# One weave instead of two for a hybrid streaming encoder step, with longer runs of value products and a sample hand-off through DRAM

## The chip, the cores and the metric

The kernel runs on one core of a Trainium2 chip. The metric is the device time of one execution in microseconds (us). Three timed executions of the kernel before gave 2235.5, 2245.63 and 2247.02 us, with a median of 2245.63 us. Engines are named as the profile names them: PE (matrix multiplies; PEld its weight loads), DVE (vector), ACT (scalar), POOL (GpSimd), SP (the queue that issues nearly all DMAs).

## The reference

One layer of a streaming encoder is computed for 2048 prompt tokens and for 8 sample streams of 16 tokens (17 blocks of 128 tokens; block 0 is the sample). Cut to what matters:

```python
h = rms_norm(x, g_in)
qkv_a, z_a, b_a, a_a, q_b, k_b, v_b, z_b, q_i, k_i, w_i, q_m, z_m = split_cols(h @ w_in)
# A: gated delta rule, 4 heads of 128, after a causal convolution; recurrent over chunks
o_a, s_new = gated_delta(q_a, k_a, v_a, g_log, beta, s0, chunk)
o_a = rms_norm(o_a, g_o) * silu(z_a)
# B: an indexer scores every admissible key, the best 256 of a query are attended to
score = einsum('bqh,bqhs->bqs', w_i, relu(einsum('bqhd,bsd->bqhs', q_i, k_i)))
_, idx = top_k(where(adm, score, -inf), 256)
o_b = softmax(q_b @ k_b[idx]) @ v_b[idx] * silu(z_b)      # the sample has 4096 cached keys a stream
# C: attention to 256 memory tokens
o_m = softmax(q_m @ mem_k) @ mem_v * silu(z_m)
y = x + concat(o_a, o_b, o_m) @ w_out
```

The outputs are y, the new convolution and recurrent states, and the new keys and values.

## The kernel before

**Order of the program.** The work is written as Python generators ("streams"). `weave` (lines 173 to 204) advances them by a clock of its own: each engine operation has an assumed cost (class `Paced`, lines 147 to 170, whose line 169 is the line under which the profile lists every compute instruction), and the stream with the smallest clock is asked for its next piece. The order in which instructions come out of this is their order of priority. The planner behind it then lays out each engine's queue: among instructions whose inputs it expects to be ready, the one that was written first goes first. An instruction of the second half can therefore stand in a queue ahead of a later-ready one of the first half. On the chip each queue runs in its order.

**First half** (`weave` at lines 1383 and 1384). `projections` multiplies the normalised input by the pieces of w_in (PSUM bank pair `pp`), group by group of three or four blocks, and writes q, k, v, gates and indexer queries to DRAM (`n_post`, `idx_post`). `stage_a`, `stage_b`, `stage_c` are the delta rule of each head and group (PSUM `pa`, `pb`, `pl`, `po`), whose results go to `mixT_d[0:512]` in DRAM; part of it is a small triangular inverse by 30 DVE steps with DMA round trips through DRAM (`blk_d`, lines 1074 to 1098). `index()` (1379) runs the memory keys, the sample's indexer and `idx_prompt` for the blocks 3 to `EARLY` - 1 = 13. After the weave the first half's pools (`b1`) are closed at line 1387.

**Second half** (`attention(True)`, lines 1695 to 1965, with a weave of its own at 1965, whose clocks begin at zero). Its pools take the memory of the closed ones: on the right side `sp` (the sample), `wo` and `op` (the output product), PSUM `py`; on the left side `kv`, `ap`, PSUM `pt`, `ps`, `po`. The right side of the first half holds what the projections use, the left side what the delta rule uses. A tile of a new pool waits for the tiles that were at its place. The streams are:

- `sample(M, sx)`: three streams. `keys_in` and `values_in` load the cached keys and values, `rows` (line 1540) goes through 72 steps of online softmax, 68 for the cache (`kind` 0) and 4 for the memory (`kind` 1). When the last of a kind is done, its result, which lies in `os_d` in DRAM, is gathered into rows by 32 small DMAs (lines 1671 to 1674), gated and written to `mix_d`. The tile for this is `work["PT"]`, which the next steps need too, and the generator stands at that place until the hand-off is over.
- `operands`, `scores`, `values`: attention of the prompt blocks 1 to 16, in order. `scores` writes exponentials into `Sm` slots; `values` (1834) transposes them four blocks at a time into PSUM `pt`, copies these to an SBUF buffer `PT` (three of them), and when three are waiting multiplies two (`visit`, 1837: four products of 128x64 by 128x128 for a buffer). `mixT` goes to `mixT_d[512:]`.
- `outputs` (1936): part 0 adds the delta rule's half of `w_out` to x and writes `part_d`; part 1 adds the attention's half and writes y. Each part loads and splits its half of w_out first (`split`, 1908), then goes through the blocks 1 to 16 and 0 at the end. A block is 24 matmuls in two PSUM banks.
- `late` (1726): `idx_prompt` for the blocks 14 to 16. When the indexer's last block is done, `more` (1730) lends its SBUF tiles to `Sm` slots and to the sample, the sample moves from PSUM `py` to the indexer's `pi`, and every other score bank is one of `pi`.

Should the selection have been inexact, the whole second half runs again (line 1980); it does not in these runs.

Of the kernel before, what the change touches and what calls it, by code (L numbers as in the profile page):

```python
# [5 lines left out]
F32 = mybir.dt.float32  # L6
# [13 lines left out]
NT = 17  # L20
# [11 lines left out]
EARLY = 14  # L32
NSEL = 256
PRI1 = (0, 0, 0, 0, 0, 0, 0, 0, 0, 0, 300, 0)
PRI2 = (0, 0, 0, 0, 0, 0, 0, 0, 0)
# [171 lines left out]
def build(tc, nc, a):  # L207
# [26 lines left out]
    os_d = dpool.tile([2, 4, 128, 64], F32, name="os_d")  # L234
    mix_d = scr("mix_d", [128, 512], F32)
# [27 lines left out]
    xpool = b1.enter_context(tc.tile_pool(name="xpool", bufs=1, side="right"))  # L263
    wpool = b1.enter_context(tc.tile_pool(name="wpool", bufs=2, side="right"))
# [21 lines left out]
    pp = b1.enter_context(tc.tile_pool(name="pp", bufs=2, space=PSUM, side="right"))  # L286
# [974 lines left out]
    np_ = b1.enter_context(tc.tile_pool(name="np", bufs=2, side="right"))  # L1261
    xp = b1.enter_context(tc.tile_pool(name="xp", bufs=XR, side="right"))
# [200 lines left out]
    class Slots:  # L1463
# [5 lines left out]
        def take(self, shape, dt, name):  # L1469
            place = self.free.pop(0)  # L1470
            return place[0].tile(shape, dt, name=name, tag=place[1], bufs=1), place
# [8 lines left out]
    def sample(M, sx):  # L1480
# [5 lines left out]
        one = M["any"]  # L1486
# [53 lines left out]
        def rows():  # L1540
# [68 lines left out]
            for j in range(n_ + 2):  # L1609
# [50 lines left out]
                if acc is not None and (c2 == 16 or kind2):  # L1660
# [7 lines left out]
                    if p2 == 3:  # L1668
                        og = work["PT"].rearrange("p a b c -> p a (b c)")
                        ot, gt = og[:, 0], og[:, 1]  # L1670
                        for h in range(4):
                            sv = os_d[kind2].rearrange("p (b h q) d -> p b h q d", b=2, h=4)[:, :, h].rearrange("p b q d -> (p b) q d")
                            for pb in range(8):
                                nc.sync.dma_start(ot[16 * pb:16 * pb + 16, 64 * h:64 * h + 64], sv[pb])  # L1674
                        nc.sync.dma_start(gt, gate_d[0:128, 256 * kind2:256 * kind2 + 256])
# [19 lines left out]
    def attention(first):  # L1695
        with ExitStack() as b3:
            nonlocal pt_, ps_, po_
            def pool(stack, name, bufs, **kw):
                return stack.enter_context(tc.tile_pool(name=name, bufs=bufs, reuse_waits="tile", **kw))
            sp = pool(b3, "sp", 1, side="right")  # L1700
            wo = pool(b3, "wo", 1, side="right")
            op = pool(b3, "op", 1, side="right")
            py = pool(b3, "py", 2, side="right", space=PSUM)
            kv = pool(b3, "kv", 1)
            ap = pool(b3, "ap", 1)
            pt_ = pool(b3, "pt", 2, space=PSUM)
            ps_ = pool(b3, "ps", 1, space=PSUM)
            po_ = pool(b3, "po", 1, space=PSUM)
            mkst = kv.tile([128, 4, 256], F32R, name="mkst")
            mvt = kv.tile([128, 2, 256], F32, name="mvt")  # L1710
            Kst = kv.tile([128, 4, 2048], F32R, name="Kst")
            Vt = kv.tile([128, 16, 256], F32, name="Vt")
            tiles = {g: {} for g in range(NT)}
            ready = []
            M = sample_tiles(sp)
            sms = Slots(*((ap, "Sm%d" % i) for i in range(NS)))
# [117 lines left out]
            def values():  # L1834


                def visit(po, nb, late, n):
                    lead = None
                    for hp, b, PT in late[:n]:
# [5 lines left out]
                        lead = ins  # L1845
                    del late[:n]

                for g in range(1, NT):
# [4 lines left out]
                    for part in range(2):  # L1853
# [3 lines left out]
                        for hp in range(2):  # L1857
# [9 lines left out]
                            for i in range(0, len(blocks), 4):  # L1867
# [7 lines left out]
                                PT = ap.tile([128, 4, 128], F32, name="PT", bufs=3)  # L1875
# [4 lines left out]
                                late.append((hp, b, PT))  # L1880
# [55 lines left out]
            def outputs():  # L1936
                for part in range(2):
                    w = yield from split(part)
                    for g in (*range(1, NT), 0):
                        rows = slice(g * 128, g * 128 + 128)  # L1940
                        if part:
                            yield from until(lambda: count["o"] >= g if g else done["smp"])
# [25 lines left out]
    attention(True)  # L1968
# [8 lines left out]
    with tc.If(clean == 0):  # L1977
        with tc.tile_pool(name="fp", bufs=2) as fp:
            exact_selection(fp)
        attention(False)  # L1980
# [33 lines left out]
```

## Time and profile before

| what | value |
|---|---|
| median of three timed executions | 2245.63 us (2235.5 to 2247.02) |
| profiled execution | 2253.76 us |
| its span, first to last instruction | 2252.0 us |
| mean granted clock of PE | 0.938 |
| DVE, ACT, POOL busy | 1661.6, 1284.3, 418.5 us |
| last projection matmul starts | 1453.0 us |
| last state of the delta rule is sent out (line 1386) | 1514.7 us |

The profile is of one execution. Busy times are sums over instructions of an engine; a matmul's end is modelled, so PE can be counted as busy while the next matmul could already start. A tile is named without its buffer number, and a name can stand for two pools (`po` is the delta rule's and later the attention's).

### The profile page before, as it was taken

What the parts mean: (1) busy time and instruction counts of PE and PEld (TensorE: products, weight loads), DVE (VectorE), ACT (ScalarE), POOL (GpSimd) and SP (SyncE); (2) the same over time, 40 slices, a digit from 0 to 9 for tenths busy, and PEclk for the clock granted to TensorE, in tenths of its full rate; (3) what the DMA queues carried; (4) which work ended last, traced back from release to release, by engine and by line L of the source; (5) the groups of instructions that cost most, each with busy time, mean ns of one, the idle gap of its engine ahead of it and who ended that gap; (6) DMA issues with size and microseconds to landing.
All of it is one profiled execution on the core that took longest, in us unless ns stands there. A gap on an engine that the chain in (4) does not pass through costs nothing.

```text
span 2252.0 us, 42965 instructions
## 1 busy us (share of the span) xinstructions
PE 1971.5 (88%) x13795; PEld 1607.3 (71%) x13795; DVE 1661.6 (74%) x6595; ACT 1284.3 (57%) x3337; POOL 418.5 (19%) x494
## 2 busy tenths in 40 slices
PE   4875978988789998999899999988999999999984
PEld 3654756877678887888788888846676666777752
DVE  5666867566888789999898999877677687655541
ACT  3455555455546566566667666557567577545430
POOL 3331423201120111111111011123211131111000
PEclk9996989889899999999899999979999999999996
DMA  7777777776544545565565755556766676765642
GB/s 236 186 228 227 269 182 214 192 253 201 185 160 158 188 164 201 207 232 187 190 230 201 244 195 189 169 176 217 246 204 219 218 228 200 242 210 185 195 139 82
DMA packets 323675, 453.21 MB, mean 201 GB/s; under 512 B 81776, under 2 KB 230896, under 8 KB 303984
## 3 DMA queue, kind: packets, MB, share of 16 engines
q1 hardware_dynamic: 323120, 449.32, 62.3%
q8 instruction: 111, 1.82, 0.3%
q0 software_dynamic: 320, 1.06, 0.2%
q14 instruction: 124, 1.02, 0.1%
HBM read 344.53 MB, written 105.75 MB: 200 GB/s over the span
## 4 chain that ended last, share of the span: by engine, by line
PE 37%; DVE 20%; DMA 6%; ACT 4%; issue 3%; SPq 1%; POOL 0%; DVEq 0%; ACTq 0%; POOLq 0%
PE py L169 10%; PE pp L169 6%; PE pt L169 5%; PE pi L169 4%; PE po L169 4%; DVE score L169 4%; PE ps L169 3%; PE pb L169 2%; DVE tmp L169 1%; PE pl L169 1%; ACT junk L169 1%; SPq L1674 1%; PE pa L169 1%; DMA svt<-in_v 1%; DVE k L169 1%
## 5 line engine op out<-in xcount | busy, mean ns | idle before, releaser
L169 PE MATMUL pp<-wh,xh 128*128 128x256 f32 (+1 forms) x952 | 292.6, 307 | 2.1 <-ACT wh L169 1.9
L169 PE MATMUL pp<-wl,xh 128*128 128x256 f32 (+1 forms) x952 | 281.3, 296 | 0.1
L169 PE MATMUL pp<-wh,xl 128*128 128x256 f32 (+1 forms) x952 | 278.6, 293 | 0.0
L169 PE MATMUL pp<-xh,wh 128*128 128x384 f32 (+1 forms) x640 | 246.7, 385 | 7.3 <-ACT q L169 4.6
L169 ACT ACTIVATE relu<-pi 128x512 f32<-128x512 f32 (+3 forms) x340 | 184.2, 547 | 107.2 <-PE pi L169 43.4
L169 PE MATMUL pp<-xl,wh 128*128 128x384 f32 (+1 forms) x640 | 239.4, 374 | 0.0
L169 PE MATMUL pp<-xh,wl 128*128 128x384 f32 (+1 forms) x640 | 238.4, 373 | 0.1
L169 DVE SCALAR_TENSOR_TENSOR score<-relu,w,score 128x512 f32<-128x512 f32 (+3 forms) x304 | 219.2, 722 | 15.5 <-ACT relu L169 7.8
L169 PEld LDWEIGHTS pp<-wh,xh 128*128 128x128 f32 x952 | 186.5, 196 | 6.7 <-issue 2.5
L169 ACT ACTIVATE junk<-score,tf 128x1024 bf16<-128x1024 f32 (+11 forms) x126 | 142.7, 1132 | 81.8 <-DVE tf L169 53.5
L169 PEld LDWEIGHTS pp<-wl,xh 128*128 128x128 f32 x952 | 186.7, 196 | 3.0 <-POOL wl L169 0.8
L169 PEld LDWEIGHTS pp<-wh,xl 128*128 128x128 f32 x952 | 186.0, 195 | 0.9
L169 PE MATMUL pi<-kstack,qst 128*128 128x512 f32 (+3 forms) x346 | 151.6, 448 | 35.7 <-DVE kstack L169 17.7
L169 POOL TENSOR_TENSOR Lm<-Lp,cf 128x256 f32<-128x256 f32 (+1 forms) x120 | 82.5, 688 | 327.1 <-PE pb L169 281.0
L169 PEld LDWEIGHTS pp<-xh,wh 128*128 128x128 f32 x640 | 125.2, 196 | 18.0 <-ACT q L169 5.6
L169 PEld LDWEIGHTS pp<-xl,wh 128*128 128x128 f32 x640 | 125.1, 195 | 9.4 <-issue 0.2
L169 PEld LDWEIGHTS pp<-xh,wl 128*128 128x128 f32 x640 | 123.6, 193 | 10.9 <-POOL wl L169 1.3
L169 PE MATMUL py<-woh,mixh 128*128 128x512 f32 x272 | 123.2, 453 | 7.4 <-ACT mixh L169 6.2
L169 PEld LDWEIGHTS pi<-kstack,qst 128*128 128x128 f32 x346 | 68.0, 198 | 67.8 <-ACT relu L169 30.1
L169 PE MATMUL py<-woh,mixl 128*128 128x512 f32 x272 | 110.8, 407 | 0.9 <-POOL mixl L169 0.9
L169 POOL TENSOR_TENSOR wl<-wr,wh 128x512 fp32r<-128x512 f32 (+1 forms) x61 | 80.6, 1330 | 164.5 <-ACT wh L169 153.8
L169 PE MATMUL py<-wol,mixh 128*128 128x512 f32 x272 | 110.5, 406 | 0.0
(428 smaller groups left out, 5352.3 us busy)
## 6 DMA issues: line engine op xcount, KB each, us to landing
skt<-in_kT SPq DMA_DIRECT2D x128, 256.0 KB
svt<-in_v SPq DMA_DIRECT2D x128, 256.0 KB
kraw<-in_kidxT SPq DMA_DIRECT2D x43, 256.0 KB
xres<-in_x SPq DMA_DIRECT2D x34, 256.0 KB
part_d<-xres SPq DMA_DIRECT2D x34, 256.0 KB
xres<-part_d SPq DMA_DIRECT2D x34, 256.0 KB
out_y<-xres SPq DMA_DIRECT2D x34, 256.0 KB
mixr<-mixT_d SPq DMA_DIRECT2D x33, 256.0 KB
```

The lines of the kernel that those rows point to most:

```text
L169: return f(*args, **kw)
L1674: nc.sync.dma_start(ot[16 * pb:16 * pb + 16, 64 * h:64 * h + 64], sv[pb])
```

## The change

The two weaves become one. `attention` now gets the first half's streams as `ahead` and weaves them together with its own. The pools of the first half are split in two stacks, `b2` (right side: projections) and `b1` (left side: delta rule). The stream `right` waits until the projections and their later steps are written out, closes `b2` and opens the second half's right pools; `left` waits for the last piece of the delta rule, sends out the two states, closes `b1` and opens the left pools. Every other stream of the second half is wrapped in `then`, which waits for its side. `index()` goes through all blocks up to 16; `late` and `EARLY` are gone.

In `values` the `PT` buffers become slots. Three are the old ones, two more are the indexer's `relu` buffers, lent when the indexer is done. When no slot is free, all waiting buffers but one are multiplied in one run: two of three as before, or four of five.

The gathering of the sample's result goes through a DRAM tile `ot_d`: four DMAs from DRAM to DRAM, one for a head, and one load of 128 rows of 1 KB take the place of 32 DMAs.

`outputs` goes through the blocks from 0 on. In part 0 the blocks 14 to 16 wait until the left side is open. If the next block is not ready (block 0 in part 1 until the sample is done), the one behind it is taken.

```diff
-    b1 = ctx.enter_context(ExitStack())
+    b1, b2 = (ctx.enter_context(ExitStack()) for _ in range(2))
...
     def index():
         yield from memory_keys(tp, pi)
         yield from idx_sample(tp, pi, SLOT)
-        yield from idx_prompt(range(3, EARLY), tp, pi, SLOT)
-    weave(tc, log, *zip((small_constants(), stage_c(), stage_b(), post(posts_t, "tp"), post(posts_n, "n"), stage_a(), splits(), loads(),
-          index(), cache_keys(), prep(xp), projections()), PRI1))
-    nc.sync.dma_start(a["pconv"], hist)
-    nc.sync.dma_start(a["pssm"].rearrange("h d e -> d h e"), Sst)
-    b1.close()
+        yield from idx_prompt(range(3, NT), tp, pi, SLOT)
...
                         for h in range(4):
-                            sv = os_d[kind2].rearrange("p (b h q) d -> p b h q d", b=2, h=4)[:, :, h].rearrange("p b q d -> (p b) q d")
-                            for pb in range(8):
-                                nc.sync.dma_start(ot[16 * pb:16 * pb + 16, 64 * h:64 * h + 64], sv[pb])
+                            nc.sync.dma_start(ot_d[kind2][:, 64 * h:64 * h + 64].rearrange("(c q) d -> c q d", q=16),
+                                              os_d[kind2].rearrange("p (b h q) d -> p b h q d", b=2, h=4)[:, :, h].rearrange("p b q d -> (p b) q d"))
+                        nc.sync.dma_start(ot, ot_d[kind2])
                         nc.sync.dma_start(gt, gate_d[0:128, 256 * kind2:256 * kind2 + 256])
...
+            def right():
+                nonlocal sp, wo, op, py
+                if first:
+                    yield from until(lambda: done["end"] and done["n"] == len(posts_n))
+                    b2.close()
...
+                done["right"] = 1
+
+            def left():
+                nonlocal kv, ap, pt_, ps_, po_, mkst, mvt, Kst, Vt, sms, pts
+                if first:
+                    yield from until(lambda: done["right"] and done["c"] == len(pieces_))
+                    nc.sync.dma_start(a["pconv"], hist)
+                    nc.sync.dma_start(a["pssm"].rearrange("h d e -> d h e"), Sst)
+                    b1.close()
...
+                pts = Slots(*((ap, "PT%d" % i) for i in range(3)))
+                done["left"] = 1
+
+            def then(side, stream):
+                yield from until(lambda: done[side])
+                yield from stream
...
-            def late():
-                if first:
-                    yield from idx_prompt(range(EARLY, NT), tp, pi, SLOT)
-
             def more():
-                yield from until(lambda: done["k"] == NT - 1)
+                yield from until(lambda: done["k"] == NT - 1 and done["left"])
                 sms.free += [(tp, "score"), (tp, "qst")]
+                pts.free += [(tp, "relu", 2)] * 2
...
-                    for hp, b, PT in late[:n]:
+                    for hp, b, (PT, place) in late[:n]:
...
                         lead = ins
+                        pts.free.append(place)
...
-                                if len(late) > 2:
-                                    visit(po, nb, late, 2)
+                                if not pts.free:
+                                    visit(po, nb, late, len(late) - 1)
...
-                    for g in (*range(1, NT), 0):
+                    left_ = list(range(NT))
+                    while left_:
+                        if part:
+                            ok = lambda g: count["o"] >= g if g else done["smp"] and done["left"]
+                        else:
+                            ok = lambda g: not first or g < 14 or done["left"]
+                        yield from until(lambda: ok(left_[0]) or len(left_) > 1 and ok(left_[1]))
+                        g = left_.pop(0 if ok(left_[0]) else 1)
...
-            weave(tc, log, *zip((more(), *sample(M, sx), values(), scores(), operands(), outputs(), late()), PRI2))
+            streams = [right(), left(), more(), *(then("right", s_) for s_ in sample(M, sx)),
+                       *(then("left", s_) for s_ in (values(), scores(), operands())), then("right", outputs())]
+            weave(tc, log, *zip(ahead, PRI1), *streams)
```

More of the change, by code (lines that the diff above doesn't have):

```diff
@@ L234, in build @@
     os_d = dpool.tile([2, 4, 128, 64], F32, name="os_d")
+    ot_d = dpool.tile([2, 128, 256], F32, name="ot_d")
     mix_d = scr("mix_d", [128, 512], F32)
@@ L285, in small_constants @@
         done["cn"] = 1
-    pp = b1.enter_context(tc.tile_pool(name="pp", bufs=2, space=PSUM, side="right"))
+    pp = b2.enter_context(tc.tile_pool(name="pp", bufs=2, space=PSUM, side="right"))
     pa = b1.enter_context(tc.tile_pool(name="pa", bufs=1, space=PSUM))
@@ L1258, in delta_c @@
         yield 1
-    np_ = b1.enter_context(tc.tile_pool(name="np", bufs=2, side="right"))
-    xp = b1.enter_context(tc.tile_pool(name="xp", bufs=XR, side="right"))
+    np_ = b2.enter_context(tc.tile_pool(name="np", bufs=2, side="right"))
+    xp = b2.enter_context(tc.tile_pool(name="xp", bufs=XR, side="right"))
     hp = b1.enter_context(tc.tile_pool(name="hp", bufs=2))
@@ L1470, in take @@
             place = self.free.pop(0)
-            return place[0].tile(shape, dt, name=name, tag=place[1], bufs=1), place
+            return place[0].tile(shape, dt, name=name, tag=place[1], bufs=place[2] if len(place) > 2 else 1), place
     def sample_tiles(sp):
@@ L1485, in sample @@
         ks, vs, masks = [], [], []
-        one = M["any"]
+        one = lambda *a, **kw: M["any"](*a, **kw)
         work = {}
@@ L1692, in sample, with attention, pool @@
         return keys_in(), values_in(), rows()
-    def attention(first):
+    def attention(first, ahead):
         with ExitStack() as b3:
             nonlocal pt_, ps_, po_
[L1698 to L1712, printed above, removed]
+            sp = wo = op = py = kv = ap = mkst = mvt = Kst = Vt = sms = pts = None
+            M = {}
+            def pool(name, bufs, **kw):
+                return b3.enter_context(tc.tile_pool(name=name, bufs=bufs, reuse_waits="tile", **kw))
+            def right():
[3 more added lines that the diff above has]
+                    b2.close()
+                sp = pool("sp", 1, side="right")
+                wo = pool("wo", 1, side="right")
+                op = pool("op", 1, side="right")
+                py = pool("py", 2, side="right", space=PSUM)
+                M.update(sample_tiles(sp))
+                done["right"] = 1
[6 more added lines that the diff above has]
+                    b1.close()
+                kv = pool("kv", 1)
+                ap = pool("ap", 1)
+                pt_ = pool("pt", 2, space=PSUM)
+                ps_ = pool("ps", 1, space=PSUM)
+                po_ = pool("po", 1, space=PSUM)
+                mkst = kv.tile([128, 4, 256], F32R, name="mkst")
+                mvt = kv.tile([128, 2, 256], F32, name="mvt")
+                Kst = kv.tile([128, 4, 2048], F32R, name="Kst")
+                Vt = kv.tile([128, 16, 256], F32, name="Vt")
+                sms = Slots(*((ap, "Sm%d" % i) for i in range(NS)))
+                pts = Slots(*((ap, "PT%d" % i) for i in range(3)))
[3 more added lines that the diff above has]
+                yield from stream
+            for n_ in ("right", "left"):
+                done[n_] = 0
@@ L1874, in values @@
                                     sms.free += [ready[j - 1 + h]["x"][0][128 * c // HALF][1] for h in range(2)]
-                                PT = ap.tile([128, 4, 128], F32, name="PT", bufs=3)
+                                pts_ = pts.take([128, 4, 128], F32, "PT")
+                                PT = pts_[0]
                                 if i // 4 % 2:
@@ L1879, in values @@
                                     S.activation(PT[:, :len(b)], pt[:, :len(b)], AF.Copy)
[L1880 removed]
+                                late.append((hp, b, pts_))
                                 yield 1
[L1882 to L1883 removed]
+                                if not pts.free:
+                                    visit(po, nb, late, len(late) - 1)
                                     yield 1
@@ L1979, in build @@
             exact_selection(fp)
-        attention(False)
+        attention(False, ())
     ctx.close()
```

13 lines of the change are left out of this document (4 added, 9 removed).

## The prediction

> **What bounds the kernel now.** I read the page first: busy shares, the slices, then the shares of the chain that ended last.
>
> ```profile
> span 2252.0 us, 42965 instructions
> ...
> PE 1971.5 (88%) x13795; PEld 1607.3 (71%) x13795; DVE 1661.6 (74%) x6595; ACT 1284.3 (57%) x3337; POOL 418.5 (19%) x494
> ...
> PE   4875978988789998999899999988999999999984
> ...
> PEclk9996989889899999999899999979999999999996
> ...
> PE 37%; DVE 20%; DMA 6%; ACT 4%; issue 3%; SPq 1%; POOL 0%; DVEq 0%; ACTq 0%; POOLq 0%
> ```
>
> PE is the busiest engine and the largest part of the chain, and its slices are full except at the start, around slices 27 and 28 and at the end. Each slice is 56 us, so these two places are near 1500 us and after 2190 us. The view of windows, cut at the last projection (1453), the start of steady attention (1545) and the attention's last matmul (2190), gives what lies there:
>
> ```profile
> core 0: us, PE busy (x) PEld busy (x) DVE busy (x) ACT busy (x) POOL busy (x), PEclk, DMA share, GB/s
> 0.00:1453.00 1453.00, 1252.67 (x7773) 1093.25 (x7774) 1147.53 (x4893) 838.71 (x2227) 290.13 (x376) 0.93 0.63 203
> 1453.00:1545.00 92.00, 73.42 (x435) 46.02 (x433) 69.20 (x246) 50.23 (x138) 27.65 (x32) 0.85 0.60 192
> 1545.00:2190.00 645.00, 622.23 (x5449) 453.42 (x5450) 435.07 (x1426) 391.11 (x961) 99.39 (x85) 0.98 0.66 210
> 2190.00:2252.00 62.00, 23.14 (x142) 14.65 (x142) 9.77 (x32) 4.23 (x11) 1.28 (x1) 0.69 0.25 75
> ```
>
> The columns are busy us of each engine, then PE's granted clock. In the middle of the second half PE has 622 of 645 us at clock 0.98: no order of the same work gains more than 23 us there. At the boundary 18.6 us are idle, and the busy 73.4 ran at 0.85, worth 11 us more. In the tail 38.9 us are idle. The first 1453 us are the same instructions in both kernels, so I give them no change.
>
> **The boundary.** The queue of SP, the row of the loads of w_out up to 1530, and the chain:
>
> ```profile
> L1915 SPq DMA_DIRECT2D xres<-in_w_out x8: 333/426/549, 1454.6 to 1492.1; - x8
> ...
> 1518.35 0.33 SPq L1257 DMA_DIRECT2D mixT_d<-oT  x1
> ...
> 1521.75 0.43 SPq L1743 DMA_DIRECT2D aqn<-mk_d  x1
> ...
> 1504.41 5.95 PE py L169 x24
> 1510.36 0.33 PE pl L169 x2
> ```
>
> The halves overlap already, since the planner lets later-written work into gaps: w_out is fetched 1.6 us after the last projection starts. The delta rule still needs until 1518.35, and only then do the left tiles come free (1521.75). What could fill PE meanwhile is the sample and part 0 of the outputs, and the first product of part 0 starts at 1504.41, because the eight loads of the split take 37.5 us through two buffers and a shared queue. The change alters none of these: the tile places, the two buffers and the delta rule's dependencies stay. It alters who goes first. Written in one weave, the split and the products of part 0 stand beside the delta rule's last pieces instead of behind them, and among themselves they no longer compete with attention pieces that can't run yet. Between nothing and the whole 18.6 + 11 = 29.6 us I take a third, **10 us**, because until about 1498 the split alone decides.
>
> This has its price on the delta rule's side. Before, its last pieces had precedence over all of the second half. A product is 5.95 us of matmuls, and the row behind it shows a delta step (`pl`) going right after one. Every load of the split and of part 0 is also moved ahead of delta-rule DMAs on SP. I take **4 us** lost, between nothing and five products' worth, 30 us (last rival).
>
> **The tail.** SP's queue, the chain and PE's order of time:
>
> ```profile
> 2183.64 0.39 SPq L1667 DMA_DIRECT2D os_d<-sO  x1
> 2184.08 14.42 SPq L1674 DMA_DIRECT2D sPT<-os_d  x31
> 2198.60 0.37 SPq L1675 DMA_DIRECT2D sPT<-gate_d  x1
> 2199.07 0.38 SPq L1905 DMA_DIRECT2D mixT_d<-mixT  x1
> ...
> 2214.66 0.34 SPq L1667 DMA_DIRECT2D os_d<-sO  x1
> 2215.10 11.93 SPq L1674 DMA_DIRECT2D sPT<-os_d  x26
> 2227.14 0.36 SPq L1675 DMA_DIRECT2D sPT<-gate_d  x1
> ```
>
> ```profile
> 2148.71 3.28 DMA mixT_d<-mixT
> 2152.04 6.16 DMA mixr<-mixT_d
> ...
> 2183.64 2.93 DMA os_d<-sO
> ...
> 2198.60 2.28 DMA sPT<-gate_d
> ...
> 2202.04 2.98 DMA mixr<-mixT_d
> ...
> 2205.10 0.64 ACT mixh L169
> ...
> 2229.98 1.77 DMA mix_d<-sPT
> ...
> 2236.72 7.71 PE py L169 x24
> ```
>
> ```profile
> 2189.87 0.44 PE L169 MATMUL pt<-cf,gate 128*128 128x128 f32 x2
> 2202.05 1.77 PE L169 MATMUL pi<-svt,sPT 128*32 128x128 f32 x14 [11.74 <-ACT sPT L169]
> ```
>
> The sample's cache steps end just before the attention does. Its first hand-off holds the tile of the next steps, and PE stands 11.74 us. The last attention result was made about 2191, but its store waits on SP behind the 31 small DMAs until 2199.07. Then come four memory steps, the second hand-off, and the product of block 0, which ends the kernel.
>
> *What a hand-off costs.* Before: from 2183.64 to 2198.60 + 2.28, 17.2 us; the second from 2214.66 to 2227.14 + 2.28, 14.8 us (six of its DMAs had gone earlier). After: the store 2.93, four issues at 14.42 / 31 = 0.465, 1.9, then the copy's landing, the load's landing, and one more issue, 0.4. No DRAM-to-DRAM copy is in the trace; the nearest landings are 1.77 and 6.16, and I take 2.28 for each, the row of the same tile. That is 9.8 us: 7.4 and 5.0 saved, **12.4 us** in all, and between 5 and 13 by the two ends for the copy. The load now stands on SP until the copy has landed, with key, value and w_out loads queued behind it; 2.3 us twice, hidden as long as two buffers of keys are ahead. [...]
>
> *What the weave does to it.* The larger effect is which work is last. The sample's streams begin when the right side opens, attention when the left does. Before, both began at clock zero of their own weave, though on the chip the left came 68 us later (1521.75 against 1453), and they ended level. In one weave that lead is written into the order, so I expect the sample, both hand-offs and the product of block 0 to be over before attention's block 16. Then only this stays behind 2190: two short copies (0.9, my estimate from the 0.64 of `mixh`), store 3.28, load 2.98, `mixh` 0.64, product 7.71, and the close from 2244.4 to 2252.0, 7.6: 23.1, and 26.3 with the longer load; I take 24. PE work moved ahead of 2190 is 23.14 - 7.71 = 15.4 us at clock 0.69, 10.8 at 0.98. Gain 62 - 24 - 10.8 = **27 us**. It contains what the faster hand-offs bring; they are not added.
>
> **The longer runs of products.**
>
> ```profile
> 2184.02 1.09 PE L169 MATMUL po<-PT,Vt 128*64 128x128 f32 x16
> ...
> 2185.63 0.66 PE L169 MATMUL po<-PT,Vt 128*64 128x128 f32 x8
> ...
> 1925.00:2190.00 265.00, 54.45 (x668) 38.84 (x668) 22.90 (x34) 29.06 (x50) 0.99 0.60 193
> ...
> L665 SPq DMA_DIRECT2D bias_d<-junk x21: 319/332/424, 573.1 to 1928.2; - x21
> ```
>
> Two runs of 8 are 1.32 us, one of 16 is 1.09: 0.23 saved on PE, which is the bound there. The two buffers are lent only when the indexer is done (its last store is at 1928.2); 668 products follow (third row, instructions on `PT` alone), 42 runs of 16. Had all been runs of 8, that is 9.7 us; the first row shows that runs of 16 occur already, since neighbours join. I take **4 us**, between 0 and 10. An earlier end of the indexer, which no longer begins a weave of its own at block 14, would lengthen this stretch and give the sample and the scores their second PSUM banks sooner; in a stretch with 23 us idle in 645 I give it nothing, and up to 10 in the range. The buffers held for longer make copies on ACT and DVE wait; both have a third of that stretch free.
>
> **Sum.** 27 + 10 + 4 - 4 = 37 off the profiled 2253.76 gives 2216.8. The profiled execution is 8.1 us above the median of 2245.63, so on the median's basis 2208.6, about **2209 us**, 1.6% faster.
>
> **Rivals.**
> - *The sample is still last.* Its steps wait for DMAs and softmax, so a lead may be eaten by the same precedence rules, and both ended level before. Then only the hand-offs and the runs count: 12.4 + 4 gives 2237.4, on the median's basis 2229. For it: the chain's tail is made of the sample. Against: 68 us of lead are more than the 62 us of the tail.
> - *The change doesn't do what it says.* The planner already interleaves the halves, as the 1.6 us show; with the same readiness the order stays, the hand-off's gain goes in the copies' landings: 5 us or less, 2241 to 2246.
> - *Everything is filled.* The whole boundary, the tail, the runs at 10 and an early indexer at 10, no loss: 27 + 29.6 + 20 = 76.6, and half of the last 49.6 would give 2193; the full sum 2169.
> - *The left side opens late, slower.* Attention may follow its own chain: `mixT_d<-mixT` goes out at 2148.71 and 2199.07 for the last two blocks, 50 us for one, and it cannot begin before the left opens. Five products of 5.95 in front of delta steps move that from 1521 to 1551; if attention keeps its pace, the end moves by 30, less the 12.4: 2263. It decides from an opening 12 us later, and is slower by over 0.5% from 24 us later. For it: the delta rule loses its precedence. Against: PE is full after 1545, so attention waits for PE and work done early is repaid.
>
> **How the numbers follow.** Forecast 0.55 (2193 to 2226); sample still last 0.17; no effect 0.08; everything filled, under 2193, 0.07; left late 0.13. The range leaves out the left-late case and the far end of the filled one, 0.16: 2176 to 2248. A measurement of this kernel tells about 0.5% (11 us) from no change: faster means under 2234.4, slower over 2256.9. Faster: 0.55 + 0.07 + 0.10 of the 0.17 = 0.72; within 0.15; slower 0.13.
>
> **What would show it.** Right: after the attention's last matmul no sample work is left, and PE is idle for under 20 us there; five DMAs at a hand-off under 10 us; runs of 16 products in most places after the indexer's end; the first product of part 0 near 1500 and the left side open before 1530. Wrong: sample steps or `mix_d` behind block 16; the first load of the attention's operands after 1540; PE below 0.95 in the middle; a first half that is longer than 1453.

## The result, and the profile after

The kernel after takes 2230.21 us in the median of nine executions (2215.68 to 2243.27), the kernel before 2245.63 in the same series. The ratio is 0.9937, with a 95% interval from 0.9915 to 0.9958: 0.6% faster, some 14 us. The forecast was 2209. The sign and the range held; the gain is less than half of the one forecast. Three of all the timed executions of this document were slow ones of 3039, 3626 and 6159 us, and count in no ratio.

The page of the kernel after, the lines that answer to those of before:

```profile
span 2226.4 us, 42886 instructions
...
PE 1943.8 (87%) x13795; PEld 1599.0 (72%) x13795; DVE 1662.9 (75%) x6595; ACT 1284.7 (58%) x3337; POOL 420.2 (19%) x494
...
PE   3866978889789998999899999968999989999995
...
PEclk9996989889899998999999999969999999999998
```

The weak end of the PE row has gone (84 became 95), but slice 27, the boundary between the halves, has sunk from 8 to 6, with a clock of 0.6 instead of 0.7. The two profiled executions differ by 25.4 us, the medians by 15.4: that of before was 8.1 above its median, that of after 1.9 below. So for the size I go by the ratios, and use the traces for the place. Three windows of each kernel, cut where the last projection matmul starts, where the left side opens (the first load of attention's operands, `aqn<-mk_d`) and at attention's last product, show the place. The columns are busy us of PE, PEld, DVE, ACT and POOL, each with its number of instructions, then PE's granted clock, the DMA engines' busy share and GB/s. First the kernel before:

```profile
1452.00:1522.00 70.00, 56.67 (x336) 34.32 (x336) 56.91 (x190) 35.50 (x103) 19.28 (x22) 0.83 0.56 179
1522.00:2190.00 668.00, 639.98 (x5555) 465.94 (x5555) 448.20 (x1486) 406.10 (x998) 107.75 (x95) 0.98 0.66 211
```

The third window is that from 2190 which the prediction shows. Then the kernel after, with the row that gives its second cut from the view of the tile `aqn`:

```profile
1448.00:1546.00 98.00, 75.16 (x478) 46.96 (x477) 75.56 (x318) 56.42 (x143) 23.32 (x25) 0.83 0.68 212
1546.00:2202.00 656.00, 611.13 (x5479) 456.94 (x5479) 422.86 (x1370) 375.68 (x939) 103.73 (x92) 0.97 0.65 207
2202.00:2226.40 24.40, 10.78 (x49) 7.67 (x45) 2.49 (x5) 1.01 (x2) 1.27 (x1) 0.79 0.27 90
```

```profile
L1762 SPq DMA_DIRECT2D aqn<-mk_d x2: 427/433/439, 1546.3 to 1547.2; - x2
```

Read length minus the first busy figure, PE's idle time. Before it is 13.3, 28.0 and 38.9 us, after it is 22.8, 44.9 and 13.6. **The tail lost 25 us of idle time, and the two stretches ahead of it took 26 up**: 80.2 us in all before, 81.3 after. The left side opened 98 us after the last projection instead of 70. What did fall is PE's busy time, from 719.8 to 697.1 us. Each kernel has one trace, and the two differ in speed by more than the medians do, so that the tests below, with four pairs of kernels, are needed to tell the causes apart.

The idle time ahead of attention's end has one large piece, 9.64 us of the 16.9 by which the middle window's idle time rose; the rest is spread over smaller waits. The order of time on PE, and the queue of SP beside it, in the kernel after:

```profile
2193.26 1.09 PE L167 MATMUL pt<-cf,mixr 128*128 128x128 f32 x4 [9.64 <-DMA mixr<-mix_d]
...
2201.52 1.09 PE L167 MATMUL po<-PT,mvt 128*64 128x128 f32 x16
```

```profile
2179.08 0.38 SPq L1661 DMA_DIRECT2D os_d<-sO  x1
2181.65 2.70 SPq L1666 DMA_DIRECT2D ot_d<-os_d  x4
2186.03 0.32 SPq L1668 DMA_DIRECT2D sPT<-ot_d  x1
2188.64 0.33 SPq L1672 DMA_DIRECT2D mix_d<-sPT  x1
2190.40 0.32 SPq L1971 DMA_DIRECT2D mixr<-mix_d  x1
```

The second hand-off now takes 9.6 us from the store of the result to the store of `mix_d` (before, 15.3 between the same ends: 2214.66 to 2229.98). But block 0's transposes stand in PE's queue ahead of block 16's last products, so PE waits 9.64 us for that hand-off (a stand of PE, as such a wait is called below) before attention can end. The sample has left the tail and waits one place earlier.

### The profile page after: what moved, and what is told of

Read it like the earlier page. It is cut to its first block, busy times and chain, and to the rows that moved or that the text cites. A ratio compares the mean times of both kernels' runs of the same rounds, so it can differ in the third digit from the quotient of the medians.

```text
span 2226.4 us, 42886 instructions
## 1 busy us (share of the span) xinstructions
PE 1943.8 (87%) x13795; PEld 1599.0 (72%) x13795; DVE 1662.9 (75%) x6595; ACT 1284.7 (58%) x3337; POOL 420.2 (19%) x494
## 5 line engine op out<-in xcount | busy, mean ns | idle before, releaser
L167 DVE SCALAR_TENSOR_TENSOR score<-relu,w,score 128x512 f32<-128x512 f32 (+3 forms) x304 | 213.4, 703 | 11.1 <-ACT relu L167 4.9
```

The source lines that it names most:

```text
L167: return f(*args, **kw)
```

## The experiments

The change has three parts: merging the weaves, the new hand-off, the lent buffers. Ratios are to the kernel before, with 95% intervals.

**First group: variants of the kernel after.** Theory A: the late opening and the stand at block 0 ate the gain. Theory B: the lent buffers hold attention back. Theory C: PE is the bound, and every delay is repaid.

`e1_block0_last`, block 0 of part 1 goes behind block 15:

```diff
-                            ok = lambda g: count["o"] >= g if g else done["smp"] and done["left"]
+                            ok = lambda g: count["o"] >= g if g else done["smp"] and count["o"] == NT - 1
```

> The changed kernel with one condition altered: in part 1 of the outputs, block 0 is taken only when attention has finished its last block (so it no longer stands in front of block 16's work in PE's queue). Theory A (the shortfall sits in queue order at two places: the left side opens 24 us late, and PE stands 9.6 us on the load of the sample's rows in front of block 16): the wait of 9.6 us is gone, and the time is 6 to 10 us under the changed kernel's 2230, ratio to before 0.989 to 0.991. Theory B (the longer runs and lent buffers made the middle emptier): no difference, 0.994. Theory C (PE is the bound and every delay is repaid): under 3 us, 0.993 to 0.994.

Measured 2227.02 us, 0.9925 [0.9900, 0.9950]. PE still waits for `mix_d`, for 8.99 us at 2203.47, now behind attention's last matmul instead of ahead of it; the tail grew from 24.1 to 32.5 us. The time is not to be told apart from that of the kernel after: this edit moves the stand and does not remove it.

`e2_delta_first`, the delta rule's three stages get a precedence of 2000 (places in the planner's order of instructions) once the projections are written out:

```diff
+            pri = e[3]() if callable(e[3]) else e[3]
+            if pri:
+                with tc.high_priority(pri):
...
-PRI1 = (0, 0, 0, 0, 0, 0, 0, 0, 0, 0, 300, 0)
+PRI1 = (0, "d", "d", 0, 0, "d", 0, 0, 0, 0, 300, 0)     # "d": 2000 * done["end"]
```

> The changed kernel with the three delta-rule streams given precedence (2000 instructions) once the projections are written out, as the two separate weaves gave them. Theory A: the left side opens 15 to 25 us earlier (operand load near 1525 instead of 1546), and the time falls by 8 to 20 us, ratio 0.985 to 0.990. Theory C: the left side opens earlier, but the time stays within 4 us, 0.992 to 0.994, since the work done meanwhile was only moved. Theory B: no difference either.

Measured 2258.46 us, 1.0064 [1.0041, 1.0088]. The left side opened at 1533.0 instead of 1546.3, and the kernel was 28 us slower: attention then needed 698 us to its last matmul instead of 656. The windows of this kernel:

```profile
1454.00:1533.00 79.00, 53.47 (x326) 34.73 (x325) 55.23 (x272) 40.07 (x106) 18.61 (x22) 0.74 0.60 180
1533.00:2231.00 698.00, 642.20 (x5627) 474.47 (x5627) 446.59 (x1409) 392.88 (x971) 107.84 (x94) 0.96 0.64 203
```

All three theories missed here, C too. The earlier opening alone was worth nothing; idle time rose to 25.5 and 55.8 us. Why block 3 in particular came late (its `mixT` was stored at 1680, in the kernel after at 1651) I could not settle; a precedence of this kind rearranges all later work in the planner's order.

`e3_both` has both edits.

> Both edits of the two runs before together. Theory A: their gains add, 15 to 30 us under the changed kernel, ratio 0.981 to 0.987. Theory C: 0.990 to 0.993, the gain of the tail alone. Theory B: 0.994.

Measured 2246.84 us, 1.0002 [0.9985, 1.0019]: all three theories missed again. Block 0 last takes some 12 us off e2, where by itself it was worth 3, not clear of nothing.

`e4_no_lent`, the lent buffers taken away, so three `PT` buffers and runs of two:

```diff
-                pts.free += [(tp, "relu", 2)] * 2
```

> The changed kernel without the two lent buffers: products run as before, two buffers of three. Theory A (with my forecast for this part): 2 to 6 us slower than the changed kernel, ratio 0.995 to 0.9965. Theory B: 5 to 15 us faster than it, 0.987 to 0.992, with less PE idle time after 1850. Theory C: the runs save PE time, so 4 us slower, 0.9955.

Measured 2244.49 us, 0.9985 [0.9965, 1.0005]. B falls. The loss of 14 us is more than A and C had for it; without the lent buffers hardly anything is left of the gain. And with A's first half fallen in e2, a new question stood: what does the merging gain at all?

**Second group: the parts alone.** `e5_handoff_alone` and `e6_lent_alone` are the kernel before with one small part each, in the lines of the diff shown above; `e9_two_weaves_all` has both; `e7_old_handoff` is the kernel after with the 32 loads put back; `e13_merge_alone` is the kernel after without both.

> The kernel before with one part of the change: a hand-off copies by four transfers into ot_d and loads that whole, instead of 32 small loads. In the kernel before the first hand-off takes 17.2 us and the second 14.8, on the chain of the tail; in the kernel after a hand-off took 9.6. If the sample bounds the tail here, as the forecast had it, both savings come out whole: 12.4 us, about 2233, ratio 0.9945, and the last attention result's store no longer stands behind 31 small loads. Rival: half of the first saving is lost because attention's last block then ends the kernel; attention's last matmul at 2190 and 23 us behind it leave no less than 2213, so this does not bind, and only a later start of work in the order that the planner makes could eat it: then 0 to 5 us.

> The kernel before with the longer runs alone: five transposed buffers, two of them lent by the indexer, and the products of four queued in one run. Forecast: 4 us (0 to 10). By the run without lent buffers in the merged kernel, 11 us. Here the indexer ends at 1928 instead of 1820, so fewer products come behind it (668 of them against some 980 at 0.9 of a block per 50 us): if the gain is in the products that follow the indexer's end, 6 to 8 us, about 2239, ratio 0.997. Rival: the gain belongs to the merged order alone (the buffers let scores go ahead while products of part 0 hold PE): then nothing, ratio 1.000.

> The kernel after with the 32 small loads of a hand-off put back. The sample stands ahead of attention's end there: its last mix_d store is at 2189, 13 us before the attention's last matmul at 2202, and the chain behind it does not wait for it. Theory: in this order a hand-off that is 7 and 5 us longer is hidden, except for the transposes of block 0 that stood 9.6 us on PE for its result; so 0 to 7 us slower than after, 2230 to 2237. Rival: the hand-off's DMAs hold up SP and with it the loads and stores of attention, all of it shows: 12 us or more, 2242 and above.

> The kernel before with both small parts, the hand-off through ot_d and the lent buffers, and its two weaves kept: everything of the change but the merging. If the merging itself gains (tail emptied of the sample, forecast 27 less 12.4 for the hand-off, plus 10 less 4 at the boundary), this stays above the kernel after: 2233 to 2238. If the merging gains nothing, as the run without lent buffers suggests (2244.5 with merging and hand-off), this is as fast as the kernel after or faster: 2225 to 2231, ratio 0.991 to 0.9935.

> The kernel after without its two small parts: the 32 loads of a hand-off put back and no lent buffers, so the merging alone. This is the one corner not yet measured of the three parts' eight combinations. If the parts add up as in the merged kernel (lent buffers 0.0048, hand-off 0.0056 of the time), the ratio is 1.004, some 2255 us: the merging alone makes the kernel slower by about 10 us. If one of the small parts gains only because the other is there, the merging alone is nearer 0.9985 to 1.000.

| | neither | hand-off | lent buffers | both |
|---|---|---|---|---|
| two weaves | 1 (before) | 0.9939 [0.9915, 0.9962] | 0.9987 [0.9964, 1.0010] | 0.9931 [0.9907, 0.9955] |
| merged | 1.0019 [0.9997, 1.0041] | 0.9985 [0.9965, 1.0005] | 0.9993 [0.9967, 1.0019] | 0.9937 [0.9915, 0.9958] (after) |

(Medians in us, first row 2233.79, 2246.15, 2231.02; second row 2252.32, 2244.49, 2245.46, 2230.21.) Read down a column: **the merging makes no kernel faster**; the differences are +0.0019, +0.0046, +0.0006 and +0.0006, and as a difference of two ratios is uncertain by some 0.003, only the second is clear of nothing, as a loss. Read along the rows: the hand-off gives 0.0061 and 0.0056 with two weaves, 0.0034 and 0.0056 merged. The hand-off alone is as fast as the whole change. The lent buffers gave 0.0013 and 0.0008 with two weaves, 0.0026 and 0.0048 merged; only the last stands out, and whether the parts need each other there is not settled.

Why the hand-off pays is in the waits of PE from 2100 on (us in total, times, longest). In the kernel before, and then with the hand-off alone:

```profile
PE pt L169 <- DMA mixr<-mix_d: 18.6, 1, 18.6
PE pi L169 <- ACT sPT L169: 11.7, 1, 11.7
```

```profile
PE pt L169 <- DMA mixr<-mix_d: 12.1, 1, 12.1
PE pi L169 <- ACT sPT L169: 4.6, 1, 4.6
```

Together 30.3 us became 16.7, which is 13.6 less; 0.0061 of 2246 us is 13.7. (The two traces themselves differ by 7.7 us, since that of e5 is of an execution 12.3 above its median.) In e7, the merged kernel with the old hand-off, the same view says:

```profile
PE pt L167 <- DMA mixr<-mix_d: 16.4, 1, 16.4
PE pi L167 <- ACT sPT L167: 8.9, 1, 8.9
```

That is 25.3 us against 9.6 after: 15.7, and the medians differ by 15.2. The other two pairs agree less well: by the same two waits 20.9 us became 14.1 from e13 to e4 (6.8; the medians differ by 7.8), and 39.2 became 14.5 from e6 to e9 (24.7, of which the wait for `mixh` took 7.5 back; the medians differ by 15.1). So the waits are where the hand-off pays, and their sum is not its exact price. The theory that a merged sample hides its hand-off (0 to 7 us) fell; it stands on PE in either order. In e6 attention's last matmul came 21.9 us earlier, at 2167.8 instead of 2189.7, but the sample's last result only 11.9 us, at 2218.1 instead of 2230.0, and by as much (11.7) the two traces differ anyway; so the lent buffers gained nothing there that can be measured.

PE's idle time after the last projection, by the same windows, shows the merging's price. It is 80.2, 70.0, 85.9 and 71.2 us with two weaves (neither, hand-off, lent, both), and 91.3, 79.9, 95.1 and 81.3 merged: **9 to 11 us more each time**. Up to the opening it is 13.3 to 13.6 with two weaves and 22.3 to 23.7 merged; that is nearly all of it. The busy time is 7 to 15 us less each time, and the count of matmuls says why: up to the start of the last projection PE has run 7772 or 7773 matmuls in each of the four kernels of two weaves, and 7798 in each of the four merged ones. Some 25 matmuls have moved ahead of it.

**Third group: what opens the left side late, and what fills the boundary.** In `e8_late_index` the indexer's blocks 14 to 16 are a stream of their own behind the right side's opening; in `e11_products_wait_left` all products of part 0 wait for the left side; `e16_late_both` has both edits. In the expectations of e8 and e11, theory A is the indexer and theory B the products of part 0.

```diff
-        yield from idx_prompt(range(3, NT), tp, pi, SLOT)
+        yield from idx_prompt(range(3, 14), tp, pi, SLOT)        # e8, e16; 14 to 16: then("right", late())
...
                     w = yield from split(part)
+                    yield from until(lambda: done["left"])          # e11, e16
```

> The kernel after with the indexer's last three blocks written as a stream of their own that starts when the right side is open, as in the kernel before. In the kernel after block 14 is scored at 1447, where before it was at 1507, and the delta rule's last head ends later. Theory A (the left side opens late because the indexer takes DVE and PE from the delta rule's last pieces): the left side opens some 75 to 85 us after the last projection instead of 98, and attention, which needs about 656 us from there to its last matmul in all kernels with lent buffers, ends 13 to 23 us earlier: 2208 to 2218, less what a later end of the indexer costs the lent buffers (to 1930 instead of 1820: up to 5). Theory B (the products of part 0 and the sample's steps do it): the opening stays at 95 to 100 us and the time at 2228 to 2235.

> The kernel after, where the products of part 0 wait for the opening of the left side; w_out is loaded and split as early as in the kernel after. Theory B (the products stand ahead of the delta rule's last matmuls on PE and of its sums on DVE): the left side opens 70 to 80 us after the last projection instead of 98. If attention's own pace sets the end (656 us from the opening to its last matmul in the kernel after and in the two-weave kernel with both small parts alike), it then ends 18 to 28 us earlier: 2202 to 2212. Rival (PE is the bound after the opening, 611 us busy of 656): the five to seven products held back, 6 us each, come behind the opening and attention ends as before: 2228 to 2240. Theory A (indexer): the opening stays at 95 to 100 and the time at 2230 or above.

> The merged kernel with both causes of the late opening taken away: the products of part 0 held until the left side opens and the indexer's last three blocks in a stream behind the right side's opening. If the two are what delays the delta rule, the left side opens 66 to 72 us after the last projection, as in the kernels of two weaves (69.0), against 98.4 in the kernel after, 83.7 with the indexer late alone and 80.5 with the products held alone. For the time, PE's account: if the idle time after the last projection comes to that of two weaves with both small parts (71 us, against 81 in the kernel after), 2226 to 2232; if the indexer's later end costs attention its pace as it did with the indexer late alone (679 us from the opening to its last matmul instead of 656), 2232 to 2240.

Measured: e8 2237.9 us, 0.9949 [0.9931, 0.9967]; e11 2226.0, 0.9914 [0.9893, 0.9934]; e16 2246.56, 1.0001 [0.9981, 1.0022]. The left side opened 83.7, 80.5 and 79.4 us after the last projection, after 98.4. Either edit brings it forward by 15 to 18 us. With both, the delta rule's last store goes out 70.8 us after the last projection (94.1 in the kernel after, 66.3 before), so these two are nearly all that delays the delta rule; but the opening then comes 8.6 us behind that store (4.3 in the kernel after), and the time is the worst of the three. None of the times follows from the opening: attention needed 679, 644 and 699 us from there to its last matmul, so the fixed 656 us of the expectations falls too. The first window of e8, up to the opening:

```profile
1450.00:1534.00 84.00, 70.89 (x453) 46.51 (x451) 64.90 (x249) 46.72 (x130) 21.62 (x23) 0.90 0.69 214
```

13.1 us idle, as with two weaves, and 7773 matmuls ahead of the last projection, as with two weaves. So it isn't the merging of delta rule, sample and part 0 that leaves the boundary empty; it is the missing of the indexer's block 14, which was PE's filler there. It isn't the only one: in e16, where block 14 is at the boundary and the products of part 0 are not, PE is idle there for 21.2 us.

```profile
1448.00:1528.00 80.00, 58.76 (x385) 36.23 (x383) 60.22 (x229) 44.16 (x125) 20.53 (x23) 0.78 0.62 187
```

Nor does the idle time of the boundary alone set the time: in e11 it is 26.7 us, more than in the kernel after, and 73.7 in all after the last projection, 7.6 less.

When the scores of block 14 are stored tells where it runs (first start of three), in the kernel before and after:

```profile
L690 SPq DMA_DIRECT2D score_d<-score x3: 319/332/332, 1506.8 to 1857.1; - x3
```

```profile
L689 SPq DMA_DIRECT2D score_d<-score x3: 326/327/332, 1447.2 to 1742.5; - x3
```

The same from the other side: `e18_index_15` is two weaves with both small parts (e9), and one more block of the indexer in the first weave, `EARLY = 15`. In `e17_index_early` it is `EARLY = NT`. Theory C of their expectations is not that of the first group: here it says that the indexer's last blocks, not the merging, emptied the boundary.

> Two weaves with both small parts, and all of the indexer's blocks in the first weave (EARLY = NT instead of 14). In the four merged kernels PE was busy 7 to 15 us less after the last projection than in their two-weave counterparts, and idle 9.2 to 11.3 us more, of which 9 to 10 before the left side opens. Theory C (it is the indexer's last blocks that moved: their PE work was done earlier, and their work no longer covers the boundary): here PE is busy some 694 to 700 us after the last projection instead of 708, the boundary is idle for some 20 us instead of 13.5, and the time is that of both small parts in two weaves, 2226 to 2236, ratio 0.991 to 0.996. Rival (the idle boundary belongs to the merging itself, to the delta rule behind the products): the boundary stays at 13 to 15 us idle, the opening at 66 to 72 us after the last projection, and the time falls to 2215 to 2224.

> Two weaves with both small parts, and one more of the indexer's blocks in the first weave (EARLY = 15 instead of 14). Under theory C a third to a half of both effects, which take each other back: 2226 to 2234. Under the rival some 4 to 6 us less than with 14: 2224 to 2228.

e18 took 2239.49 us, 0.9969 [0.9954, 0.9985]. Its three windows:

```profile
1458.00:1534.00 76.00, 53.96 (x334) 34.33 (x333) 59.56 (x281) 43.31 (x114) 20.10 (x23) 0.75 0.64 194
1534.00:2171.00 637.00, 615.12 (x5505) 457.69 (x5505) 426.06 (x1370) 383.73 (x956) 105.31 (x94) 0.99 0.69 216
2171.00:2238.40 67.40, 28.32 (x167) 17.85 (x163) 11.75 (x40) 4.83 (x13) 1.27 (x1) 0.64 0.31 93
```

Without any merging the boundary is now idle for 22.0 us instead of 13.6 in e9, PE busy 697.4 us after the last projection instead of 707.8: the merged kernel's two marks (22.8 and 697.1), from one number changed; 7799 matmuls stand ahead of the last projection. Even the longest waits of PE at the boundary (1445 to 1535) are the same three, in e18 and then in the kernel after:

```profile
PE pb L169 <- ACT Y L169: 3.2, 1, 3.2
PE py L169 <- DMA skt<-in_kT: 3.1, 1, 3.1
PE py L169 <- DVE bd L169: 3.0, 1, 3.0
```

```profile
PE py L167 <- DVE bd L167: 3.5, 1, 3.5
PE pb L167 <- ACT Y L167: 3.2, 1, 3.2
PE py L167 <- DMA skt<-in_kT: 2.8, 1, 2.8
```

In e9, with block 14 at the boundary, the longest is one inside the indexer, and of these three only the one for `bd` is there, with 1.2 us:

```profile
PE pi L169 <- ACT relu L169: 4.3, 6, 2.8
```

So theory C holds for the boundary, though e18 was slower than expected of it, by 5 us; its tail was 67 us against 54 in e9. e17 took 2302.38 us, 1.0251 [1.0224, 1.0279], and tells little: with the indexer written out beforehand, the sample used the indexer's PSUM banks from its first step on and began at 1668, not 1457.

**Fourth group: the sample moved.** `e10_memory_first` (two weaves, both small parts) and `e12_merged_memory_first` (the kernel after) put the four memory steps ahead of the cache steps. `e14_left_and_sample` is e11, and `e15_sample_first` is e9, with a precedence of 300 for the sample's streams. The first pair of lines is the edit of e10 and e12, the second that of e15; e14 sets the same 300 in its list of streams.

```diff
-        steps = [(0, p, c) for p in range(4) for c in range(17)] + [(1, p, 0) for p in range(4)]
+        steps = [(1, p, 0) for p in range(4)] + [(0, p, c) for p in range(4) for c in range(17)]
...
-PRI2 = (0, 0, 0, 0, 0, 0, 0, 0, 0)
+PRI2 = (0, 300, 300, 300, 0, 0, 0, 0, 0)
```

> The kernel before with both small parts (two weaves), and the sample's four memory steps put ahead of its 68 cache steps instead of behind them; what is computed is the same. In the two-weave kernel attention's last matmul is at 2170 and the end at 2224; PE stood 14.0 us for the second hand-off, at the end of the memory steps. With these gone from the end, the last hand-off starts with the fourth cache part, at 2169 to 2178, and its result is stored 10 us later, at 2179 to 2188 instead of 2203: 15 to 24 us less, so 2207 to 2216. Rival: the order that the planner makes from this puts the sample's last steps later, since its steps are paced against attention's: 2222 to 2231.

> The kernel after with the memory steps first. There PE stood 9.6 us at block 0's transposes for the second hand-off's result (16.4 with the old hand-off, which also cost 8.9 at a sample step, and the kernel was 15 us slower). If that stand is all that the sample still costs, it goes, and the time is 9 to 10 us less: 2219 to 2222. Rival: attention's own chain sets the end, and a PE that stands for 9.6 us beside it costs less than that: 2225 to 2231.

> The merged kernel with the products of part 0 held until the left side opens, and in addition a precedence of 300 for the sample's three streams. With the products held, the left side opened 80 us after the last projection instead of 98 and attention's last matmul came at 2176 instead of 2202, but the sample's last hand-off was stored only at 2200 and ended the kernel at 2222. Theory (two chains end the kernel, and what counts is the later): with the sample some 12 to 20 us earlier and attention no more than 8 later, the end is at about 2208 to 2214: 2212 to 2218 us. Rival (PE's order is full: what goes earlier pushes other work later by as much): attention's last matmul moves by what the sample gains or more, 2225 to 2240.

> The kernel before with both small parts (two weaves), and a precedence of 300 for the sample's three streams in the second weave. There attention's last matmul is at 2170, the last hand-off is stored at 2203, and the end is at 2224. Theory (the sample ends this kernel, attention has some 30 us to spare): an order in which the sample goes first moves the last hand-off to 2180 to 2190 and the end to 2205 to 2212, 2212 to 2219 us. Rival: precedence takes PE and DVE from the delta rule's last pieces and from attention by as much as it gives, 2228 to 2240.

Measured: e10 2229.09 us, 0.9909 [0.9884, 0.9934]; e12 2239.83, 0.9967 [0.9948, 0.9986]; e14 2262.78, 1.0075 [1.0048, 1.0102]; e15 2274.49, 1.0127 [1.0097, 1.0158]. Four misses: e10 came out as its rival has it, the others slower than either case. With the memory steps early, the last `mix_d` went out at 2209 in e10 (2203 in e9) and at 2216 in e12 (2189 after): the cache steps seem to have spread out over the time that had come free. With precedence, the left side opened 115 us after the last projection in e14 and 76 in e15, as the sample's steps went ahead of the delta rule's (PE ran 602 matmuls up to the opening in e14, 320 in e11), and the last `mix_d` went out later, at 2235 and 2240 (in e11 and e9 at 2200 and 2203). What sets the pace of the sample's steps is left open.

No variant is clearly faster than the kernel after. The best, e10, e11 and e1 with 0.9909 to 0.9925, have intervals that hold its 0.9937 or nearly reach it.

## Why the prediction was right in sign and wrong in size

The forecast counted 27 - 12.4 + 10 - 4 = 20.6 us for the merging itself, and measured beside both small parts it gave nothing (0.0006 of the time, 1.3 us, as a loss). What was measured is the hand-off and the lent buffers. The result, 2230, lies outside the 2193 to 2226 of the case that was forecast, and one of its own signs of being wrong came: the first load of attention's operands went out after 1540, at 1546.3.

- **First half, no change.** Wrong in a way that mattered. "The same instructions in both kernels" overlooked that without `EARLY` the indexer's block 14 no longer waits for the second weave. It ran ahead of the last projection: its scores were stored from 1447.2 instead of 1506.8, and 7798 matmuls stand ahead of that projection instead of 7773.
- **Boundary, 10 us gained and 4 lost.** This step failed. PE's idle time there rose by 9.5 us, and the left side opened 29 us later, counted from the last projection. The forecast took the filler at the boundary to be the sample and part 0, and said that the change alters none of it; there was a third filler, block 14 of the indexer, and the change took it away. e8 and e18 show this from both sides. What the boundary lost, PE had already done: it was busy 7 to 15 us less afterwards. By these sums the two take each other back, and the merging ends at nothing.
- **Tail, 27 us.** The picture was right (24 us behind attention's last matmul forecast, 24.1 measured), to the microsecond by luck, since the first short copies and the store's issue took 3.7 us (2202.3 to 2206.02) where 0.9 was put, and the close 6.1 where 7.6 was put; the gain was wrong. It was counted as gain that PE's idle time leaves the tail. It did, but in PE's queue block 0's transposes went ahead of block 16's products, and the stand for the hand-off, 9.64 us, came with them. The forecast asked whether the sample's *work* would be done ahead of 2190, not whether its *latency* would be hidden there.
- **Hand-off, 12.4 us**, inside the 27. Right: 0.0061 of the time alone, 13.7 us. Between the forecast's own ends, the store and the load's landing, the second hand-off took 9.0 us (2179.08 to 2186.03 + 2.07) and the first 10.4 (2147.87 to 2156.21, and the same 2.07 as an estimate), against a forecast of 9.8 for each: 5.7 and 6.8 saved where 5.0 and 7.4 were forecast. (The first one's `mix_d` still came 15.05 us after its store, 18.0 before.) The two landings of the way through `ot_d` are in the chain of the kernel after, 4.3 us against 4.6 in the forecast (2.28 for each):

```profile
2183.72 2.24 DMA ot_d<-os_d
2186.03 2.07 DMA sPT<-ot_d
```

Both were issued on SP. The way through `ot_d` pays by far against 32 issues, of which 31 took 14.42 us in the kernel before.

- **Longer runs, 4 us, between 0 and 10.** With two weaves 0.0013 of the time, 2.9 us, not clear of nothing; in the merged kernel with the new hand-off 0.0048, 10.8 us, at the end of the range.
- **The rivals.** "The sample is still last" gave 2229 from hand-off and runs alone, and 2230 was measured: not because the sample is last (its `mix_d` went out 13.7 us ahead of attention's last matmul), but because what is left of the sum when the merging gives nothing is the same sum. That is luck for this rival. "The left side opens late" happened, by 24.5 us on the clock of the span, and attention ended 12.6 us later (2202.3 against 2189.7); the kernel wasn't slower, since the tail behind it was 38 us shorter.

## What to carry to other kernels

Count PE's idle time over the whole stretch that a reordering can touch, not over the window that it empties: here 25 us left the tail, and 26 came back ahead of it. Before merging two schedules, name the work that fills each gap now and check that it still comes at that time; and ask where in PE's queue the wait for a late result stands: here it was 9.64 us ahead of attention's end and 8.99 behind it in e1, at times that can't be told apart. When a change has several parts, time the cheapest alone first: the hand-off alone was as fast as the whole change.

## What the runs showed of the hardware

By an estimate from the trace, one stand of PE cost more than its length. Windows of the kernel after around the 6.94 us for which PE waits for block 16's result:

```profile
2205.00:2212.70 7.70, 0.29 (x3) 0.09 (x2) 1.03 (x3) 1.01 (x2) 0.00 (x0) 0.79 0.52 166
2212.70:2216.30 3.60, 3.47 (x7) 2.32 (x8) 0.00 (x0) 0.00 (x0) 1.27 (x1) 0.51 0.02 5
2216.30:2220.00 3.70, 3.70 (x18) 3.00 (x16) 0.69 (x1) 0.00 (x0) 0.00 (x0) 1.00 0.22 79
```

For 3.6 us after the stand the granted clock is 0.51 and 7 matmuls start; then it is 1.00, and the same matmuls start every 0.23 us (17 from 2216.31 to 2219.94; the count of 18 holds one begun before). Seven take 1.6 us at that pace, so the stand cost an estimated 2.0 us beyond its own 6.94. After the stand of 9.64 us the clock is 0.50 in the first 3.6 us (2193.2 to 2196.8), 0.67 in the next 3.6, and 1.00 from 2200.4 to 2202.7. That the stands lower the clock is my reading; no run varies their length alone.
